# Samples' states as moving operands, head sums in column groups, rates in row halves: one change to the RWKV stage of a hybrid decoder step

## The chip, the core and the metric

The kernel runs on one core of one Trainium2 chip. The metric is the device time of one execution, in microseconds; the median of three runs of the kernel before is 1292.83 us (1290.94 to 1293.05). The engines are TensorE (PE, its weight loads shown as PEld), VectorE (DVE), ScalarE (ACT), GpSimd (POOL) and SyncE (SP), which issues most loads. Each engine takes its instructions in the order in which the program has them.

## The reference

Two layers, each a half SwiGLU block, a mixer and a second half SwiGLU block; the first mixer is RWKV-7, the second RetNet. There are 256 prompt rows and 8 sample rows (one new token each, with its own stored state), together 264 columns, and 16 heads of 64. The change lies in the RWKV mixer:

```python
kk = hd(k * k_k)
kk = kk / jnp.maximum(jnp.sqrt(jnp.sum(kk * kk, axis=-1, keepdims=True)), 1e-12)   # lengths
w_log = -softplus(-(w0 + jnp.tanh(xw @ w1) @ w2)) - 0.5                            # rates
a = sigmoid(a0 + (xa @ a1) @ a2)                                                   # rates
def step(S, inp):                      # S: value x key, one per sequence and head
    sa = jnp.einsum('bhvk,bhk->bhv', S, -kk_t)
    S = S * d_t + sa[..., None] * (kk_t * a_t) + v_t[..., None] * k_t
    return S, jnp.einsum('bhvk,bhk->bhv', S, r_t)
y = head_norm(y) * lnx_g + lnx_b
y = y + jnp.sum(r_h * k_h * r_k, axis=-1, keepdims=True) * v_h                     # bonus sums
```

## The kernel before

Activations lie with the 1024 channels on partitions: eight tiles `f` of 128 channels (two heads) by 264 columns. Weights stream from memory in units of eight 128x128 tiles. Outside the RWKV mixer each unit is split into two float32r parts (`hi` on ACT, `lo` on DVE) and a product takes three float32r matmuls (`mm3`, line 251). In the mixer the weights of k, r and v are used whole in float32, where one matmul is two records in the trace.

`weave` (line 204) runs the main `stream` and a list of side generators against a small model of engine clocks, and the tile scheduler then sets each engine's final order. In `rwkv` (line 464) the stream makes k, r and v (products `xk`, `xr`, `xv`), then the output product. Beside it run: `lengths` (707), sums of squares over a head, for four tiles a call; `rates` (721), which makes decay and `a` from 64 hidden rows each; `stage` (753), which spreads the lengths back over channels and makes `al`, `be`, `ka`; `inverse` (796), a DVE chain that inverts the 32x32 blocks of all heads and starts when every tile's `A` is there; `prep` (842), which makes the bonus products `bon` (tile `rc`) after the inverse; `heads2` (867), chunk products for two tiles a call; and `decode` (1034), the eight samples.

In `decode` each of 64 states (tile f and sample b, two heads each, value on one axis and key on the other) is the stationary operand and two columns of `dq` move (line 1058): 128 matmuls, 64x64 weights, two columns. The states come in four loads of 512 KB on POOL's queue into tiles of the tag `big`, three buffers, which `selT`, `V` and `tm` of the inverse use before them.

A sum over a head is a float32 matmul with a 0/1 matrix: `hsel` gives 16 rows (one a head) for the lengths, `selT` spreads them over 128 rows (763), `bones` sums and spreads at once for the bonus (947).

Of the kernel before, what the change touches and what calls it, by code (L numbers as in the profile page):

```python
# [10 lines left out]
F32 = mybir.dt.float32  # L11
F32R = mybir.dt.float32r
# [6 lines left out]
KT = D // 128  # L19
# [22 lines left out]
class Step:  # L42
# [158 lines left out]
    def mark(self, key):  # L201
        self.done[key] = self.now
# [242 lines left out]
class Rwkv(Step):  # L445
    def rw_consts(self, p):

        nc = self.nc
        c = p.tile([128, NCST], F32, name="cst")
        nc.scalar.dma_start(c, self.io["cst"])  # L450
        self.ident = c[:, CST["ident"]:CST["ident"] + 128]
        self.bones = c[:, CST["bones"]:CST["bones"] + 128]
        self.hsel = c[:, CST["hsel"]:CST["hsel"] + 128].rearrange("p (f h) -> p f h", f=KT)
# [7 lines left out]
        self.diag = col("diag", 4)  # L461
        self.rst = col("rst", 256)

    def rwkv(self, gain):
# [6 lines left out]
        with ExitStack() as ctx:  # L471
# [8 lines left out]
            same = dict(vT="mx", yl="lw", z2="kkn", z0="ta")  # L480

            def tmp(name, n=T, bufs=2):
                tag = same.get(name, name)
                return P.tile([128, n if tag in ("bs", "mv", "sd4", "nm4") else SLOT], F32, tag=tag, name=name, bufs=bufs)[:, 0:n]

            def parts(x, where="mm"):
                h, l = (slot("part", T, F32R) if w == "m" else
# [14 lines left out]
            selT = big("selT")[0:16].rearrange("p (f n) -> p f n", f=KT)  # L502
            nc.scalar.dma_start(selT, self.io["selT"])

            X = P1.tile([128, 32, 64], F32, name="X")
            for p0 in (32, 96):
# [131 lines left out]
            def heads():  # L638
                for p in range(KT // 2):
                    self.beside(TU["head"] + TU["headf"] * p, heads2(p))  # L640
                self.beside(TU["decode"], decode())

            def mixes(name, mu):
                if TU["wait_" + name]:
# [62 lines left out]
            def lengths(g, sqs):  # L707
                yield f"k{g}"
                ssq = ps_()
                for j in range(4):  # L710
                    self.mm(ssq[0:16, 0:T], self.hsel[:, 4 * g + j, :], sqs[j], j == 0, j == 3)
                rn = tmp("mx")[0:16]
                self.act(rn, ssq[0:16, 0:T], AF.Sqrt)
                self.ts(rn, rn, 1e-12, None, ALU.max)
                rnr[g] = slot("rnr")[0:16]
                self.vec("reciprocal", rn, out=rnr[g])
                mark(f"rn{g}")
                yield


            def rates():
                yield "hid"
                for f in range(KT):
                    s_ = st[f]
                    wh, wl = wa2[f]
                    (th, tl) = hid[0]
                    zw, za = ps_()[:, 0:T], ps_()[:, 0:T]
                    for z, p0 in ((zw, 0), (za, 64)):
# [24 lines left out]
            def stage(f):  # L753
# [88 lines left out]
            def prep(f):  # L842
# [11 lines left out]
                mark(f"bon{f}")  # L854
                yield

            def values(f, pv):
# [9 lines left out]
            def heads2(p):  # L867
# [74 lines left out]
                Ta = [c64(t[:, 256:448], NC - 1) for t in WT]  # L942

                for f, s_ in zip(fs, s2):
                    yield f"bon{f}"
# [88 lines left out]
            def decode():  # L1034
# [16 lines left out]
                Ss = [load(i) for i in range(3)]  # L1051
                yield 8.0
                po = ps_()[:, 0:128].rearrange("p (n q) -> p n q", q=2)
                for i in range(4):
                    for n in range(16):
                        f, b = divmod(16 * i + n, NS)
                        for e in range(2):
                            self.mm(po[own(e), 16 * i + n], Ss[i][own(e), n], dq[own(e), 1:5:3, f, b], behind=(n, e) != (0, 0))
                    if i == 0:
                        Ss.append(load(3))  # L1060
                    if i == 2:
                        yield 4.0
                self.act(fl(1), po[:, :, 0])
# [6 lines left out]
                self.tt(y[:, 0], y[:, 0], po[:, :, 1], ALU.add)  # L1070
# [55 lines left out]
    return slice(NV * i, NV * i + NV), slice(NV * i * 64, NV * (i + 1) * 64)  # L1126


NM = 60
NW = 10  # L1130
TU = dict(PEF=1.0, DVEF=1.0, ACTF=1.5, LP=0.5, LD=0.12, LA=0.15, SLACK=0.2, AHEAD=1, wk='mm', wr='mm', wv='mm', IL=8, pin_stream=0, pin_hidden=1, pin_rates=0, pin_mixes=0, pin_lengths=0, pin_stage=0, pin_inverse=0, pin_prep=1, pin_head=0, pin_saved=0, vp='r7', hv=0, hw=1, hidden=8, rates=7, mixr=1, mixv=5, inverse=0, saved=4, prep=3, head=2, headf=0.01, decode=9, lengths=3, stage=7, by_step=0, HE=0, wait_r=None, wait_v='k0', PW=4, SW=8, RK=3, INVY=8, pre=3.5, n0=3, n1=4)
WHOLE = "krv"
SLOT = 266


CST = {}
_c = 0
for _k, _w in (("ident", 128), ("bones", 128), ("hsel", 128), ("m_ak", 64), ("m_up", 64), ("eye2", 64), ("centre", 128),
               ("rows64", 64), ("back", 256), ("diag", 4), ("rst", 256)):
    CST[_k] = _c  # L1140
    _c += _w
NCST = _c
# [2 lines left out]
def consts():  # L1145
# [11 lines left out]
    hs = np.zeros((128, KT, 16))  # L1157
    for f in range(KT):
        hs[p, f, 2 * f + h] = 1
    put("hsel", hs.reshape(128, 128))  # L1160

    put("m_ak", q[:, None] < s)
    put("m_up", q[:, None] <= s)
# [9 lines left out]
    put("rows64", r64.reshape(128, 64))  # L1173
    put("back", bk.reshape(128, 256))
    put("diag", p[:, None] // 32 == np.arange(4)[None, :])
    r = np.ones((128, 4, 64))
    r[:, :, 0] = 0
    put("rst", r.reshape(128, 256))
    sel = np.zeros((16, KT, 2, 64), np.float32)
    for f in range(KT):  # L1180
        for e in range(2):
            sel[2 * f + e, f, e] = 1
    return c, sel.reshape(16, KT, 128)


def pack_wkv(s):
# [363 lines left out]

# [34 lines left out]
```

## Time and profile before

| | us |
|---|---|
| median of three runs | 1292.83 |
| the profiled execution | 1295.7 |
| its span | 1293.9 |
| PE busy in the span | 1266.0 |
| DVE busy | 850.0 |
| ACT busy | 673.8 |

A row of a timeline gives start, duration, engine, line, operation, output and inputs, and how many records are merged; the durations of neighbours overlap, so what a block costs is the distance from its start to the start of the next. The column PEclk in the windows is the granted clock of TensorE as a share of its full 2.4 GHz; 0.50 is its lower level, 1.2 GHz. The RWKV mixer lies between about 200 and 430 us.

### The profile page before, as it was taken

The numbers are of one execution on the slowest core, as the hardware profiler recorded it, in microseconds if no ns is written. First come the engines' busy times: TensorE is split into PE (matmuls) and PEld (weight loads), VectorE is DVE, ScalarE is ACT, GpSimd is POOL, SyncE is SP. The second block draws the span as 40 slices with busy tenths as digits, with TensorE's granted clock in tenths as the row PEclk, the third lists the DMA queues.
The fourth block names the chain that finished last, engine by engine and source line by source line (L and its number), as shares of the span: only waits on it lengthen the run. The fifth ranks groups of instructions, "written<-read, shape, count | busy, mean of one in ns | idle before, by whom it ended". The sixth has DMA issues, their size and how long they took to land.

```text
span 1293.9 us, 29072 instructions
## 1 busy us (share of the span) xinstructions
PE 1266.0 (98%) x12186; PEld 1197.3 (93%) x12186; DVE 850.0 (66%) x1391; ACT 673.8 (52%) x1167; POOL 67.3 (5%) x169
## 2 busy tenths in 40 slices
PE   9999999999998999999999999999999999999996
PEld 9999998678787999999999999988888799999996
DVE  6766567589235787765566665577878866666554
ACT  6544442653434677764456454445765554544542
POOL 0000001131100000000000000011111100000000
PEclk9999999999879999999999999999999999999998
DMA  7656554333400467665558555669879655555552
GB/s 233 181 181 185 181 170 137 99 116 115 147 7 23 153 219 222 211 195 182 178 179 279 183 181 182 204 236 329 312 269 334 213 194 180 179 180 179 179 180 83
DMA packets 66755, 239.09 MB, mean 185 GB/s; under 512 B 7504, under 2 KB 8912, under 8 KB 66496
## 3 DMA queue, kind: packets, MB, share of 16 engines
q1 hardware_dynamic: 59472, 212.63, 51.1%
q0 software_dynamic: 6544, 23.40, 4.9%
q8 instruction: 95, 1.56, 0.5%
q10 hardware_dynamic: 608, 1.21, 0.2%
q14 instruction: 36, 0.29, 0.1%
HBM read 214.86 MB, written 22.35 MB: 183 GB/s over the span
## 4 chain that ended last, share of the span: by engine, by line
PE 91%; DVE 4%; DMA 2%; ACT 2%; issue 1%; DVEq 0%; SPq 0%; ACTq 0%
PE ps L138 90%; DMA S<-in_ret 1%; DVE V L105 1%; DVE tm L105 1%; PE ps L153 1%; DMA rcst<-in_rcst 1%; DVE lo L105 0%; ACT X L90 0%; ACT L90 0%; ACT hi L90 0%; DMA raw<-in_w 0%; DVE KQ L105 0%; DVE xf L105 0%; ACT sd L90 0%; DVE sd L126 0%
## 5 line engine op out<-in xcount | busy, mean ns | idle before, releaser
L90 ACT ACTIVATE hi<-raw 128x1024 fp32r<-128x1024 f32 (+1 forms) x344 | 362.8, 1055 | 440.4 <-PE ps L138 207.9
L105 DVE TENSOR_TENSOR lo<-raw,hi 128x1024 fp32r<-128x1024 f32 (+1 forms) x344 | 418.5, 1217 | 233.6 <-ACT hi L90 232.3
L138 PE MATMUL ps<-ah,hi 128*128 128x264 f32 (+1 forms) x1824 | 522.9, 289 | 1.0 <-ACT ah L90 1.0
L138 PE MATMUL ps<-al,hi 128*128 128x264 f32 (+1 forms) x1824 | 517.1, 285 | 0.0
L138 PE MATMUL ps<-ah,lo 128*128 128x264 f32 (+1 forms) x1824 | 514.3, 285 | 0.0
L138 PEld LDWEIGHTS ps<-ah,hi 128*128 128x128 f32 x1824 | 342.8, 189 | 9.1 <-issue 7.4
L138 PEld LDWEIGHTS ps<-al,hi 128*128 128x128 f32 x1824 | 343.7, 189 | 4.1 <-issue 2.9
L138 PEld LDWEIGHTS ps<-ah,lo 128*128 128x128 f32 x1824 | 342.3, 189 | 0.1
L138 PE MATMUL ps<-hh,hi 128*128 128x264 f32 x832 | 237.2, 285 | 0.0
L138 PE MATMUL ps<-hl,hi 128*128 128x264 f32 x832 | 237.0, 285 | 0.0
L138 PE MATMUL ps<-hh,lo 128*128 128x264 f32 x832 | 236.8, 285 | 0.0
L138 PEld LDWEIGHTS ps<-hl,hi 128*128 128x128 f32 x832 | 156.8, 188 | 0.0
L138 PEld LDWEIGHTS ps<-hh,lo 128*128 128x128 f32 x832 | 156.7, 188 | 0.0
L138 PEld LDWEIGHTS ps<-hh,hi 128*128 128x128 f32 x832 | 156.4, 188 | 0.1
L105 DVE TENSOR_TENSOR h<-s,ps 128x264 f32<-128x264 f32 x88 | 37.1, 428 | 49.7 <-PE ps L138 48.3
L105 DVE TENSOR_TENSOR t<-ps,rs 128x264 f32<-128x264 f32 x88 | 37.2, 431 | 20.2 <-PE ps L138 19.9
L114 DVE SCALAR_TENSOR_TENSOR S<-ps,ks,S 128x512 f32<-128x512 f32 x64 | 45.0, 743 | 6.2 <-PE ps L138 6.2
L90 ACT ACTIVATE S<-S 128x1024 f32<-128x1024 f32 x32 | 33.8, 1056 | 14.3 <-DMA S<-in_ret 14.1
L105 DVE TENSOR_TENSOR hl<-h,hh 128x264 fp32r<-128x264 f32 x88 | 37.0, 427 | 0.3
L90 ACT ACTIVATE hh<-h 128x264 fp32r<-128x264 f32 x88 | 35.3, 408 | 3.6 <-DVE h L105 3.6
L90 ACT ACTIVATE s<-t 128x264 f32<-128x264 f32 x88 | 35.2, 409 | 2.2 <-DVE t L105 2.1
L138 PE MATMUL ps<-part,hi 128*128 128x264 f32 (+1 forms) x176 | 34.5, 309 | 0.0
(261 smaller groups left out, 1214.6 us busy)
## 6 DMA issues: line engine op xcount, KB each, us to landing
raw<-in_w SPq DMA_DIRECT2D x363, 512.0 KB, 3.6
S<-in_ret SPq DMA_DIRECT2D x32, 512.0 KB, 5.8
out_sret<-S POOLq DMA_DIRECT2D x32, 512.0 KB, 3.8
dS<-in_wkvt POOLq DMA_DIRECT2D x4, 512.0 KB, 4.4
Sd<-in_wkv SPq DMA_DIRECT2D x4, 512.0 KB, 4.7
out_swkv<-Sd POOLq DMA_DIRECT2D x4, 512.0 KB, 4.0
out_pret<-so POOLq DMA_DIRECT2D x8, 256.0 KB, 2.3
rcst<-in_rcst SPq DMA_DIRECT2D x1, 1100.0 KB, 6.9
```

The source lines that it names most:

```text
L90: ins = self.nc.scalar.activation(out=out, in_=in_, func=func, scale=scale, **kw)
L105: ins = self.nc.vector.tensor_tensor(out=out, in0=a, in1=b, op=op)
L114: ins = self.nc.vector.scalar_tensor_tensor(out=out, in0=a, scalar=s, in1=b, op0=op0, op1=op1)
L138: ins = self.nc.tensor.matmul(out=out, lhsT=lhsT, rhs=rhs, start=start, stop=stop)
L153: self.nc.tensor.transpose(out, in_, ident)
```

## The change

Four edits. `lengths` and the new `bonuses` sum squares and bonus products of four tiles into four 32-row column groups of one output (`rows64`, 128x32 weights) and keep the sums as two float32r parts; `to_heads` spreads them back with two float32r matmuls of 32 rows (`spread`), where `selT` and `bones` did it in float32. `rates` alternates its six float32r matmuls between the upper and the lower 64 rows. In `decode` the state is now the moving operand (64 columns), and the weight is a 64x32 tile of `kkr` that holds the two vectors of one state in its own two columns and zeros elsewhere; 16 states are added up in one output, four such outputs lie in four column groups, and `pick` turns the result back. The states pass in two halves of two loads each; `kkr` takes the third `big` buffer and `selT` is gone.

```diff
+            spread = P1.tile([128, 128], F32R, name="spread")
+            self.act(spread, self.back[:, 0])
+            def sums(out, xs):
+                for j, x in enumerate(xs):
+                    self.mm(out[32 * j:32 * j + 32, 0:T], self.rows64[:, 0], x, behind=j > 0)
+            def to_heads(out, rows, j):
+                s = slice(32 * j, 32 * j + 32)
+                for i, x in enumerate(rows):
+                    self.mm(out, spread[s], x[s], i == 0, i == 1)
...
                 ssq = ps_()
-                for j in range(4):
-                    self.mm(ssq[0:16, 0:T], self.hsel[:, 4 * g + j, :], sqs[j], j == 0, j == 3)
+                sums(ssq, sqs)
...
+                self.vec("reciprocal", rn, out=rn)
+                rnr[g] = parts(rn, "aa")
...
-                    for z, p0 in ((zw, 0), (za, 64)):
-                        s = slice(p0, p0 + 64)
-                        self.mm(z, wh[s], th[s], True, False)
-                        self.mm(z, wh[s], tl[s], False, False)
-                        self.mm(z, wl[s], th[s], False, True)
+                    for i, (w, t) in enumerate(((wh, th), (wh, tl), (wl, th))):
+                        for z, p0 in ((zw, 0), (za, 64)):
+                            s = slice(p0, p0 + 64)
+                            self.mm(z, w[s], t[s], i == 0, i == 2, behind=i + p0 > 0)
...
-                self.mm(rb, selT[:, f, :], rnr[f // 4])
+                to_heads(rb, rnr[f // 4], f % 4)
...
+            def bonuses(g):
+                for j in range(4):
+                    yield f"bon{4 * g + j}"
+                pr = ps_()
+                sums(pr, [st[4 * g + j]["bon"] for j in range(4)])
+                h, l = tmp("bh", T, 2, F32R), tmp("bl", T, 2, F32R)
+                self.act(h, pr[:, 0:T], scale=64.0)
+                self.stt(l, pr[:, 0:T], 64.0, h, ALU.mult, ALU.subtract)
...
-                    self.mm(pbo, self.bones, s_["bon"])
+                    to_heads(pbo, bonus[f // 4], f % 4)
...
-                        for e in range(2):
-                            self.mm(po[own(e), 16 * i + n], Ss[i][own(e), n], dq[own(e), 1:5:3, f, b], behind=(n, e) != (0, 0))
+                for h in range(2):
+                    K = big("kkr")
+                    nc.gpsimd.memset(K, 0.0)
+                    Ss = [load(2 * h + j) for j in range(2)]
+                    for q in range(2):
+                        nc.gpsimd.tensor_copy(K.rearrange("p (j n) -> p j n", j=2)[:, :, q:512:34],
+                                              fl(1 + 3 * q)[:, 32 * h:32 * h + 32].rearrange("p (j n) -> p j n", j=2))
+                    K = K.rearrange("p (j n m) -> p j n m", j=2, m=32)
+                    yield TU["dS"]
+                    pr = ps_()[:, 0:64]
                     for n in range(16):
+                        for j in range(2):
+                            for e in range(2):
+                                g = 64 * j + 32 * e
+                                self.mm(pr[g:g + 32], K[own(e), j, n], Ss[j][own(e), n], n == 0, n == 15, behind=(n, j, e) != (0, 0, 0))
+                    self.act(y[:, h], pr)
+                    yield 0.2
+                    for e in range(2):
+                        self.mm(po[own(e), :, 32 * h:32 * h + 32], y[:, h], self.pick[:, e])
```

The schedulers put many instructions elsewhere. TensorE's order around the end of the inverse, before (`tm,AT` is the inverse's first product, `PI,ka` and `cst,vt` belong to the first two tiles of `heads2`):

```order
L138 MATMUL ps<-cst,al 64x64 x24
L138 MATMUL ps<-xv,raw 128x264 x25
L138 MATMUL ps<-tm,AT 32x32 x32
L138 MATMUL ps<-xv,raw 128x264
L138 MATMUL ps<-PI,ka 64x64 x16
L138 MATMUL ps<-cst,vt 64x64 x16
```

and now:

```order
L138 MATMUL ps<-cst,al 64x64 x24
L138 MATMUL ps<-xv,raw 128x264
L138 MATMUL ps<-PI,ka 64x64 x16
L138 MATMUL ps<-cst,vt 64x64 x16
L138 MATMUL ps<-xv,raw 128x264 x17
L138 MATMUL ps<-rc,cst 32x264 x4
L138 MATMUL ps<-xv,raw 128x264 x4
L138 MATMUL ps<-tm,AT 32x32 x32
```

The first bonus sums (`rc,cst`) now stand ahead of the inverse's first product, with four value products between them. Before the last `be,al` block 48 of the 64 `xr` products now stand, where 40 stood.

TensorE's order around the samples' states, before (`G,Ls` and `Ly,G` are the chunk recurrence, `dq,dS` the states):

```order
L138 MATMUL ps<-al,ka 64x64 x16
L138 MATMUL ps<-pp,ka 64x64 x16
L138 MATMUL ps<-dq,dS 64x2 x96
L138 MATMUL ps<-G,Ls 64x64 x4
L138 MATMUL ps<-Ly,G 64x64 x4
L138 MATMUL ps<-rc,cst 128x264
L138 MATMUL ps<-PI,be 64x64 x16
```

and now:

```order
L138 MATMUL ps<-dS,kkr 32x64 x64
L138 MATMUL ps<-z,X 64x64 x16
L138 MATMUL ps<-aT,X 64x64 x12
L138 MATMUL ps<-al,ka 64x64 x16
L138 MATMUL ps<-pp,ka 64x64 x16
L138 MATMUL ps<-cst,yd 64x2x32 x2
L138 MATMUL ps<-G,Ls 64x64 x4
L138 MATMUL ps<-Ly,G 64x64 x4
L138 MATMUL ps<-bh,spread 128x264
L138 MATMUL ps<-bl,spread 128x264
L138 MATMUL ps<-PI,be 64x64 x16
```

The states stand ahead of the second head pair's products instead of behind them, and come as 64 and 64 matmuls instead of 96 and 32.

POOL's order from the last gather on, now (before, the first load stood where the first memset stands, and each of the other three loads waited for its own buffer):

```order
L1081 MEMSET kkr 128x1024
L1084 COPY kkr<-dq 128x2x16 x2
L110 TENSOR_TENSOR PI<-cst,PL 128x256 x4
L696 COPY dq<-vt 128x8 x6
L1073 DMA dS<-in_wkvt 128x1024
L696 COPY dq<-vt 128x8 x2
L1073 DMA dS<-in_wkvt 128x1024
L110 TENSOR_TENSOR PI<-cst,PL 128x256 x2
L1081 MEMSET kkr 128x1024
L1073 DMA dS<-in_wkvt 128x1024 x2
L1084 COPY kkr<-dq 128x2x16 x2
```

The first load takes the buffer of `tm`, the second that of `V`, whose last reader is the inverse's last product (`V,AT`). The second memset and the last two loads wait for the first 64 matmuls.

## Rows read from the trace of the kernel before

**Rows 1.** The page: busy time of each engine, and the chain that ended last

```profile
PE 1266.0 (98%) x12186; PEld 1197.3 (93%) x12186; DVE 850.0 (66%) x1391; ACT 673.8 (52%) x1167; POOL 67.3 (5%) x169
...
PE 91%; DVE 4%; DMA 2%; ACT 2%; issue 1%; DVEq 0%; SPq 0%; ACTq 0%
```

**Rows 2.** Windows: stretch, us, busy PE PEld DVE ACT POOL, PEclk, DMA share, GB/s

```profile
250.00:282.00 32.00, 32.00 (x460) 22.56 (x459) 28.87 (x74) 23.63 (x64) 14.18 (x43) 1.00 0.22 71
...
348.00:349.00 1.00, 0.33 (x6) 0.33 (x8) 0.00 (x0) 0.00 (x0) 0.00 (x0) 0.70 0.31 123
...
349.00:365.00 16.00, 16.00 (x289) 14.47 (x287) 1.81 (x7) 0.66 (x2) 1.79 (x3) 0.50 0.12 36
...
369.00:372.00 3.00, 3.00 (x111) 2.88 (x107) 2.40 (x12) 0.00 (x0) 0.00 (x0) 0.50 0.01 3
...
423.00:428.00 5.00, 5.00 (x25) 4.76 (x26) 3.72 (x8) 1.69 (x3) 0.00 (x0) 0.66 0.00 0
...
440.00:490.00 50.00, 50.00 (x411) 49.93 (x410) 39.80 (x56) 39.20 (x95) 0.54 (x1) 1.00 0.67 214
```

**Rows 3.** TensorE's timeline, samples' states: start, us, what, records, idle before

```profile
348.67 10.40 PE L138 MATMUL ps<-dq,dS 64*64 64x2 f32 x191 [2.29 <-issue]
...
358.83 0.77 PE L138 MATMUL ps<-G,Ls 64*64 64x64 f32 x8
...
365.99 1.98 PE L138 MATMUL ps<-dq,dS 64*64 64x2 f32 x64
```

**Rows 4.** DVE's timeline, either end of the inverse's chain

```profile
283.84 1.97 DVE L132 STREAM_TRANSPOSE A<-Ag 128x1024 f32<-128x1024 f32 x1 [1.41 <-ACT Ag L90]
...
318.17 1.71 DVE L114 SCALAR_TENSOR_TENSOR rc<-rc,par,k 128x264 f32<-128x264 f32 x4
```

**Rows 5.** TensorE's timeline, from the value products to the second head pair

```profile
307.30 11.39 PE L138 MATMUL ps<-xv,raw 128*128 128x264 f32 x50
...
318.62 1.20 PE L138 MATMUL ps<-tm,AT 32*32 32x32 f32 x64
...
336.48 1.16 PE L138 MATMUL ps<-rc,cst 128*128 128x264 f32 x4
...
344.40 0.69 PE L138 MATMUL ps<-z,X 64*64 64x64 f32 x32
```

**Rows 6.** TensorE's timeline, a block of 64x32 weights and its successor

```profile
254.69 0.73 PE L138 MATMUL ps<-be,al 64*32 64x32 f32 x48
...
255.35 0.71 PE L138 MATMUL ps<-rnr,selT 16*128 16x264 f32 x2
```

**Rows 7.** POOL's timeline, two loads of the states

```profile
336.86 0.53 POOL L1048 DMA_DIRECT2D dS<-in_wkvt  x1 [0.74 <-PE ps L138]
...
352.55 0.59 POOL L1048 DMA_DIRECT2D dS<-in_wkvt  x1 [6.94 <-PE ps L138]
```

**Rows 8.** Tile dS, its loads

```profile
DMA to landing us min/median/max: 4.2/4.4/5.2
```

**Rows 9.** Line 799, a memset of 128x1024 on POOL: duration ns min/median/max

```profile
L799 POOL MEMSET V<- x1: 963/963/963, 204.5 to 204.5; 128x1024 f32 x1
```

**Rows 10.** TensorE's timeline, one bonus sum and its successor

```profile
381.63 0.71 PE L138 MATMUL ps<-rc,cst 128*128 128x264 f32 x2
...
382.28 0.69 PE L138 MATMUL ps<-PI,be 64*64 64x64 f32 x32
```

**Rows 11.** TensorE's timeline, lengths' sums and one pair of rates

```profile
240.70 1.96 PE L138 MATMUL ps<-sq,cst 128*16 128x264 f32 x8
...
242.59 1.60 PE L138 MATMUL ps<-xk,raw 128*128 128x264 f32 x6
...
263.33 0.51 PE L138 MATMUL ps<-part,hi 64*128 64x264 f32 x4
...
263.90 0.71 PE L138 MATMUL ps<-rnr,selT 16*128 16x264 f32 x2
```

More of the change, by code (lines that the diff above doesn't have):

```diff
@@ L461, in rw_consts @@
         self.diag = col("diag", 4)
+        self.pick = col("pick", 128).rearrange("p (e q n) -> p e q n", e=2, q=2)
         self.rst = col("rst", 256)
@@ L478, in slot, with tmp @@
                 return P.tile([128, SLOT], dt, tag=tag, name=name, bufs=bufs or NM)[:, 0:n]
-            same = dict(vT="mx", yl="lw", z2="kkn", z0="ta")
-            def tmp(name, n=T, bufs=2):
+            same = dict(z2="kkn", z0="ta", bh="kkn", bl="ta")
+            def tmp(name, n=T, bufs=2, dt=F32):
                 tag = same.get(name, name)
-                return P.tile([128, n if tag in ("bs", "mv", "sd4", "nm4") else SLOT], F32, tag=tag, name=name, bufs=bufs)[:, 0:n]
+                return P.tile([128, SLOT], dt, tag=tag, name=name, bufs=bufs)[:, 0:n]
             def parts(x, where="mm"):
@@ L641, in heads @@
                 self.beside(TU["decode"], decode())
+                self.beside(TU["prep"], bonuses(0), bonuses(1))
             def mixes(name, mu):
@@ L709, in lengths @@
                 ssq = ps_()
-                for j in range(4):
-                    self.mm(ssq[0:16, 0:T], self.hsel[:, 4 * g + j, :], sqs[j], j == 0, j == 3)
-                rn = tmp("mx")[0:16]
-                self.act(rn, ssq[0:16, 0:T], AF.Sqrt)
+                sums(ssq, sqs)
+                rn = tmp("mx")
+                self.act(rn, ssq[:, 0:T], AF.Sqrt, scale=64.0)
                 self.ts(rn, rn, 1e-12, None, ALU.max)
-                rnr[g] = slot("rnr")[0:16]
-                self.vec("reciprocal", rn, out=rnr[g])
+                self.vec("reciprocal", rn, out=rn)
+                rnr[g] = parts(rn, "aa")
                 mark(f"rn{g}")
@@ L855, in prep @@
                 yield
+            bonus = [None, None]
+            def bonuses(g):
[6 more added lines that the diff above has]
+                self.stt(l, pr[:, 0:T], 64.0, h, ALU.mult, ALU.subtract)
+                bonus[g] = h, l
+                mark(f"bonus{g}")
+                yield
             def values(f, pv):
@@ L944, in heads2 @@
                 for f, s_ in zip(fs, s2):
-                    yield f"bon{f}"
+                    yield f"bonus{f // 4}"
                     pbo = ps_()[:, 0:T]
-                    self.mm(pbo, self.bones, s_["bon"])
+                    to_heads(pbo, bonus[f // 4], f % 4)
                     self.tt(s_["bon"], pbo, s_["vt"])
@@ L1049, in load @@
                     return S
[L1051 to L1054, printed above, removed]
-                    for n in range(16):
-                        f, b = divmod(16 * i + n, NS)
-                        for e in range(2):
-                            self.mm(po[own(e), 16 * i + n], Ss[i][own(e), n], dq[own(e), 1:5:3, f, b], behind=(n, e) != (0, 0))
[L1059 to L1063, printed above, removed]
+                po = ps_()[:, 0:128].rearrange("p (q n) -> p q n", q=2)
+                for h in range(2):
[8 more added lines that the diff above has]
+                    pr = ps_()[:, 0:64]
+                    for n in range(16):
+                        for j in range(2):
[6 more added lines that the diff above has]
+                        self.mm(po[own(e), :, 32 * h:32 * h + 32], y[:, h], self.pick[:, e])
+                self.act(fl(1), po[:, 0])
                 pbr = ps_()[:, 0:128].rearrange("p (q n) -> p q n", q=2)
@@ L1126, in part_of @@
     return slice(NV * i, NV * i + NV), slice(NV * i * 64, NV * (i + 1) * 64)
-NM = 60
+NM = 61
 NW = 10
-TU = dict(PEF=1.0, DVEF=1.0, ACTF=1.5, LP=0.5, LD=0.12, LA=0.15, SLACK=0.2, AHEAD=1, wk='mm', wr='mm', wv='mm', IL=8, pin_stream=0, pin_hidden=1, pin_rates=0, pin_mixes=0, pin_lengths=0, pin_stage=0, pin_inverse=0, pin_prep=1, pin_head=0, pin_saved=0, vp='r7', hv=0, hw=1, hidden=8, rates=7, mixr=1, mixv=5, inverse=0, saved=4, prep=3, head=2, headf=0.01, decode=9, lengths=3, stage=7, by_step=0, HE=0, wait_r=None, wait_v='k0', PW=4, SW=8, RK=3, INVY=8, pre=3.5, n0=3, n1=4)
+TU = dict(PEF=1.0, DVEF=1.0, ACTF=1.5, LP=0.5, LD=0.12, LA=0.15, SLACK=0.2, AHEAD=1, wk='mm', wr='mm', wv='mm', IL=8, pin_stream=0, pin_hidden=1, pin_rates=0, pin_mixes=0, pin_lengths=0, pin_stage=0, pin_inverse=0, pin_prep=1, pin_head=0, pin_saved=0, vp='r7', hv=0, hw=1, hidden=8, rates=7, mixr=1, mixv=5, inverse=0, saved=4, prep=3, head=2, headf=0.01, decode=9, lengths=3, stage=7, by_step=0, HE=0, wait_r=None, wait_v='k0', PW=4, dS=5.0, SW=8, RK=3, INVY=8, pre=3.5, n0=3, n1=4)
 WHOLE = "krv"
@@ L1137 @@
 _c = 0
-for _k, _w in (("ident", 128), ("bones", 128), ("hsel", 128), ("m_ak", 64), ("m_up", 64), ("eye2", 64), ("centre", 128),
-               ("rows64", 64), ("back", 256), ("diag", 4), ("rst", 256)):
+for _k, _w in (("ident", 128), ("bones", 128), ("m_ak", 64), ("m_up", 64), ("eye2", 64), ("centre", 128),
+               ("rows64", 64), ("back", 256), ("diag", 4), ("pick", 128), ("rst", 256)):
     CST[_k] = _c
@@ L1156, in consts @@
     put("bones", h[:, None] == h[None, :])
[L1157 to L1160, printed above, removed]
     put("m_ak", q[:, None] < s)
@@ L1175, in consts @@
     put("diag", p[:, None] // 32 == np.arange(4)[None, :])
+    pk = np.zeros((2, 2, 2, 8, 2, 2, 2, 2, 2, 8))
+    for j, e, i, b, q in np.ndindex(2, 2, 2, 8, 2):
+        pk[j, e, i, b, q, e, q, j, i, b] = 1
+    put("pick", pk.reshape(128, 128))
     r = np.ones((128, 4, 64))
@@ L1178, in consts @@
     put("rst", r.reshape(128, 256))
[L1179 to L1183, printed above, removed]
+    return c
 def pack_wkv(s):
@@ L1552 @@
     inp = {k: np.asarray(v) for k, v in inputs.items()}
-    cst, selT = consts()
+    cst = consts()
     rcst = ret_consts()
@@ L1556 @@
         x=pack_x(np.concatenate([inp["x_prompt"][0], inp["x_sample"][:, 0]], 0)),
-        par=pack_par(inp), cst=cst, selT=selT, rcst=rcst,
+        par=pack_par(inp), cst=cst, rcst=rcst,
         shift=pack_x(inp["state_rwkv_shift"][0]),
```

5 lines of the change are left out of this document (1 added, 4 removed).

## The prediction

> **What bounds the kernel now.** I read first the page's engine table and its chain: TensorE is busy 98% of the span and carries 91% of the chain that ended last [rows 1]. Time is won only where TensorE has less to do, waits less or runs at a better clock. All edits lie in the RWKV mixer, so next come the windows there. TensorE has its full clock nearly everywhere, 411 float32r matmuls of 264 columns in 50 us, or 0.12 us each, but from 349 to 365 us the granted clock is 0.50, the lower level of 1.2 GHz, again from 369 to 372, and 0.66 in the mean of 423 to 428 [rows 2]. TensorE's timeline says what stands there: behind an idle time of 2.3 us, 191 records of the samples' states take 10.2 us, and 64 more come at 365.99 [rows 3]. The third view is DVE's: busy for 28.9 of the 32 us from 250 to 282 [rows 2], then in the inverse's chain from 283.84 on, and only at 318.17 does it begin the four bonus products `rc` that follow the inverse [rows 4]. TensorE's row there reads as a tie: value products run without a gap from 307.30 to 318.62, and the inverse's first product follows at once [rows 5]. So up to 318 us two chains are about equally late, TensorE's and DVE's, and behind that TensorE is alone.
>
> **The samples' states.** Before, they take 346.20 (348.67 less the 2.3 idle and a first record of 0.2) to 358.83, 12.6 us, and 2.0 at 365.99: 14.6 us [rows 3]. After, there are 128 matmuls, 256 records, with 64x32 weights and 64 moving columns on four quarters of the array. The nearest row is the block `be,al`, also 64x32 weights on the same quarters, 48 records in 0.66 us, start to start, 13.8 ns each [rows 6]: 3.5 us for 256. It moves only 32 columns; I take 15 ns, 3.8 us. The other end is the states' own price at full clock, 64 records in 1.98 us, 31 ns [rows 3]: 7.9 us. The turning back by `pick`, four small products, I put at 0.5 us in all. So 4.3 us against 14.6.
>
> Two statements of the Trainium skill speak against 15 ns. TensorE: Matmul & The Clock Gate, section Back-to-back issue gap, gives matmuls of 1 to 64 columns about 60 cycles each, some 25 ns; 256 of them would be, as an estimate from that page, 6.4 us. TensorEngine Tiling (Array Packing), Gotcha 1, says that row tiles may not use one PSUM bank at once, and both row halves of the new product write one bank; by that rule pairs would run in turn, near the 31 ns end. The block `be,al` does the same, both halves into one bank, and took 13.8 ns a record [rows 6], so the trace agrees with neither.
>
> **The new waits for loads.** The first two loads are issued ahead of the first half, the second of them into the buffer of `V`, which the inverse's last product frees. Before, such a load was issued 0.4 us after that product's end (336.48, then 336.86) [rows 5, 7], and it lands 4.4 us after issue, 4.2 to 5.2 [rows 8]: 4.8 us. TensorE's work in between is four spreads at 0.12 [rows 2] and the first pair's 0.85 and 2.0 us of chunk products, 3.3 us. It waits 1.5 us (1.3 to 2.3), and all of `heads2` queues behind it, since TensorE is strictly in order. The second half waits longer: only after the first half does POOL clear `kkr`, 0.96 us [rows 9], and issue two loads at 0.55 [rows 7], so the last one lands 0.1 + 0.96 + 1.1 - 0.55 + 4.4 plus some sharing, 6.0 to 7.4 us, I take 7.0, after the first half's end. TensorE has meanwhile 1.8 us of the second pair's products and what stood between 358.83 and 365.99: 7.2 us at half clock [rows 3], 3.6 at full, less two bonus sums at 0.65 [rows 10], plus four spreads, 0.5, and `pick`. That is 4.9 us; the wait is 2.1 (1.1 to 2.5).
>
> **Lengths, spreads, rates.** A float32 sum costs 0.47 us (four in 1.89, 240.70 to 242.59) [rows 11]. In four column groups side by side four cost about one, so `lengths` saves 1.4 us on its first call; in its second other products stand between, and I count nothing. Eight spreads by `selT` have the columns of a bonus sum, 0.65 us [rows 10], and become two of 0.12 each: 8 x 0.41, 3.3 us. Six matmuls of a rate take 0.57 us, 263.33 to 263.90 [rows 11]; in alternating halves three times 0.12, 8 x 0.21, 1.7 us (none if the halves take turns). TensorE sheds 6.4 us before the inverse starts.
>
> What of that reaches the end? DVE is nearly full there [rows 2], and the first spread comes 1.4 us plus three rates, 2.0 us, sooner, so the inverse starts about 2.0 us earlier (1.4 to 2.9: DVE also gets one more subtraction for each call of `lengths`, 0.4 us as a quarter of the `rc` row [rows 4]). TensorE meanwhile runs ahead of it. The reordered queue puts 54 products of `xr` and `xv` between the last `be,al` and the first bonus sums, where 65 stood ahead of the inverse's first product: 11 x 0.453 (25 in 11.32 [rows 5]) is 5.0 us less, 1.2 us of `PI,ka` and `cst,vt` more. So TensorE reaches those sums at 318.62 - 3.8 - 2.0 = 312.8, but all four `rc` are ready at 318.17 + 1.71 - 2.0 = 317.9 [rows 4]. It stands idle 5 us with the inverse's product queued behind. An idle of 2.3 us went ahead of the drop at 348.7 [rows 2, 3], so I expect half clock when it resumes; in the dense products of 423 to 428 a drop lost 5 x 0.34 = 1.7 us [rows 2].
>
> From there: before, 318.62 to 344.40 where the second pair's products begin [rows 5], 25.8 us, of which 0.6 is idle. After: less two bonus sums (1.0 us), plus four spreads (0.5), two grouped sums (0.9), three `xv` (1.4), less 1.2 done already: 25.8 us. So 317.9 + 25.8 + 1.7 = 345.4, 1.0 later than the like point before. The 6.4 us are gone, eaten by the idle time.
>
> **The sum.** After: 345.4, wait 1.5, first half 1.9, work 4.9, wait 2.1, second half 1.9, hence 357.7; before the same work ends at 365.99 + 1.98 = 368.0. That is 10.3 us. The half clock of 369 to 372 should be gone, 1.5 us [rows 2]. Four later bonus sums go from 0.65 to 0.24, 1.6 us; TensorE has gaps there, so I count 0.8. Together 12.6 us off the profiled execution: 1295.7 - 12.6 = 1283.1. That execution, span 1293.9 plus 1.8 around it, stands 2.9 us above the median, so in the median's terms 1280.2, and I say 1280. What follows is feed-forward work at TensorE's pace, where a start that is earlier by so much ends earlier by as much. The constants and the extra slot of `NM` I cost at nothing: they issue nothing of their own.
>
> **Rivals.**
> - The clock holds at the long wait, or the waits for loads are short: the 1.7 us come back, and up to 3 of the waits. For it: behind the idle time of 346 stood products of two columns, so the idle alone need not have been the cause. Against it: 5 us is over twice as long. 1275.5 to 1278.5.
> - The clock falls at the first load wait and stays down over the samples' stage, as it did for 16 us before [rows 2]. The 8.7 us of work there double, the second wait of 2.1 vanishes: 6.6 us lost, 1286.6. Against it: the new products are denser.
> - The tiles take turns, so that the change doesn't do what it says: 31 ns for the states, 4.1 us, and bonus sums at four times 0.47, 2.9 us: 1287. `be,al` speaks against it [rows 6]. Slower rates alone would only shorten the idle 5 us.
> - The slower side: the 5 us stall at the bonus sums puts the clock down, and the small products behind it, cut up by the waits for loads, don't bring it back before the second half is done. All 34.5 us of work from 317.9 on then cost double; the waits vanish (3.6) and the 1.7 counted already fall out: 29 us, 1309. It decides once the half level costs over 14.4 us of work, some 29 us on end. The longest stretch so far is 16, under products of two columns.
>
> **Chances.** Forecast 0.55 (1278.5 to 1284, its term bounds); better 0.13; half clock at the samples 0.13; tiles in turn 0.10; slower side 0.04; 0.05 for a loss that I don't see and that leaves the time as it was. Range: 1275 to 1288, which takes in the first three rivals but for their ends. A measurement here tells 0.2%, 2.6 us, from no change. Faster 0.89, same 0.06, slower 0.05.
>
> **What would show it.** In the profile after: an idle time of TensorE of some 5 us ahead of `rc,cst` with 32 rows, released by DVE's `rc`; half clock just behind it; `dS,kkr` in two blocks of 128 records, 1.9 us each, with 1.5 and 2.1 us of waiting for loads ahead; full clock at 369 to 372 less 10. The forecast is wrong if the blocks take 4 us each, if the clock in the samples' stage is 0.50, or if the inverse starts later than 283 us.

## The result: 0.75% slower, and what the profile after shows

The changed kernel takes 1301.58 us (median of four, 1299.79 to 1303.49) against 1292.03; the ratio is 1.0075 with the 95% interval [1.0061, 1.0090]. The forecast was 1280, in a range of 1275 to 1288; the change went the other way. The profiled execution took 1302.58 us, span 1300.8, against 1293.9 before. The page after, the engines' busy time and the chain that ended last, answers [rows 1]:

```profile
PE 1259.2 (97%) x12210; PEld 1189.6 (91%) x12210; DVE 849.4 (65%) x1395; ACT 675.6 (52%) x1174; POOL 69.9 (5%) x175
...
PE 90%; DVE 4%; DMA 2%; ACT 1%; issue 1%; DVEq 0%; SPq 0%; POOL 0%; ACTq 0%
```

TensorE works 6.8 us less and the span is 6.9 us longer: 13.7 us more idle time. The windows of [rows 2] after, and one that is new (310 to 320):

```profile
250.00:282.00 32.00, 29.84 (x455) 21.81 (x455) 26.68 (x69) 22.43 (x60) 12.24 (x38) 1.00 0.24 70
310.00:320.00 10.00, 7.13 (x80) 6.16 (x81) 9.51 (x24) 1.78 (x2) 0.00 (x0) 0.83 0.18 52
349.00:365.00 16.00, 9.90 (x381) 8.80 (x381) 3.09 (x10) 3.07 (x9) 3.52 (x7) 0.89 0.40 134
369.00:372.00 3.00, 2.44 (x127) 2.21 (x128) 1.52 (x7) 0.22 (x1) 0.00 (x0) 1.00 0.02 5
```

From 250 to 282 and from 349 to 365 us TensorE had no idle time before; now it has 2.2 and 6.1 us, though from 349 to 365 the half clock is nearly gone (0.89 instead of 0.50). Ahead of the inverse, TensorE's timeline had this row for the last `be,al` before:

```profile
282.64 0.73 PE L138 MATMUL ps<-be,al 64*32 64x32 f32 x48
```

Now, ahead of and behind the inverse, answering [rows 5, 6]:

```profile
255.41 0.73 PE L138 MATMUL ps<-be,al 64*32 64x32 f32 x48 [1.68 <-DVE be L114]
...
281.08 0.51 PE L138 MATMUL ps<-part,spread 32*128 32x264 f32 x2
281.52 0.73 PE L138 MATMUL ps<-be,al 64*32 64x32 f32 x48
282.18 3.83 PE L138 MATMUL ps<-xr,raw 128*128 128x264 f32 x16
285.94 0.73 PE L138 MATMUL ps<-be,al 64*32 64x32 f32 x48
...
312.87 0.89 PE L138 MATMUL ps<-PI,ka 64*64 64x64 f32 x26 [3.01 <-DVE M L105]
...
314.65 8.71 PE L138 MATMUL ps<-xv,raw 128*128 128x264 f32 x34
323.29 0.65 PE L138 MATMUL ps<-rc,cst 128*32 128x264 f32 x8
323.87 2.05 PE L138 MATMUL ps<-xv,raw 128*128 128x264 f32 x8
325.85 1.20 PE L138 MATMUL ps<-tm,AT 32*32 32x32 f32 x64
...
343.96 1.20 PE L138 MATMUL ps<-V,AT 32*32 32x32 f32 x64
345.09 0.39 PE L138 MATMUL ps<-bh,spread 32*128 32x264 f32 x2
```

DVE's timeline, answering [rows 4]:

```profile
287.14 1.98 DVE L132 STREAM_TRANSPOSE A<-Ag 128x1024 f32<-128x1024 f32 x1 [2.94 <-ACT Ag L90]
...
320.72 1.70 DVE L114 SCALAR_TENSOR_TENSOR rc<-rc,par,k 128x264 f32<-128x264 f32 x4
```

The last `be,al` comes 3.3 us later than before, and so does the inverse. TensorE then stops at `PI,ka` for an `M` that stands inside the inverse's chain on DVE, resumes at less than full clock (0.83 in that window), and reaches `tm,AT` 7.2 us later than before, 5.1 behind the start of `rc` where it was 0.5. `V,AT` ends 8.6 us later (345.09, before 336.48). The samples' stage on TensorE's timeline, answering [rows 3]:

```profile
353.07 0.28 PE L138 MATMUL ps<-M,WT 64*64 64x64 f32 x3 [4.11 <-issue]
...
354.81 3.20 PE L138 MATMUL ps<-dS,kkr 64*32 64x64 f32 x124 [0.94 <-DMA dS<-in_wkvt]
...
360.44 0.46 PE L138 MATMUL ps<-pp,ka 64*64 64x64 f32 x14 [0.65 <-issue]
...
365.97 0.68 PE L138 MATMUL ps<-cst,al 64*64 64x64 f32 x16 [1.41 <-issue]
366.58 1.77 PE L138 MATMUL ps<-dS,kkr 64*32 64x64 f32 x112
369.52 0.43 PE L138 MATMUL ps<-dS,kkr 64*32 64x64 f32 x16 [1.17 <-issue]
...
372.87 0.46 PE L138 MATMUL ps<-cst,vt 64*64 64x64 f32 x17 [0.91 <-issue]
```

The states end at 369.9, 2.0 us later than before. The first block of 124 records took 3.1 us (354.81 to 357.95), the second 1.8 for 112: behind the gap of 4.11 and the wait for the load the clock had fallen to its half level.

```profile
354.80:357.40 2.60, 2.59 (x100) 2.59 (x104) 0.00 (x0) 0.01 (x1) 0.00 (x0) 0.50 0.00 0
```

From 336 to 430 us, idle time that no row releases ("issue") sums to 11.3 us in 9 pieces, against 2.7 in 2. The pieces have a beat: 126, 128 and 127 matmul records lie between the gaps that end at 360.44, 365.97, 369.52 and 372.87, each with its weight load. The profile's DMA table has a queue of kind "instruction":

```profile
q8 instruction: 96, 1.57, 0.5%
```

That is 16.4 KB a packet, or some 65 bytes for each of the 252 to 256 records between two gaps. The trace also has the time of each packet. The nine gaps end 1.2 to 1.5 us behind the end of a q8 packet: the gap that ends at 365.97 behind a packet that ended at 364.64, for instance, and the one at 369.52 behind 368.23. The same holds for all 84 such gaps from 336 to 430 us in the twenty traces of this case, with 1.2 to 1.6 us, and the 2.29 us ahead of the states before is one of them (348.67, packet 347.41). So "issue" is here TensorE waiting for its instructions. In 345 to 350 us, ahead of the gap of 4.11, the table for that stretch has no row for q8 (no packet starts between 344.55 and 350.74), and the weight queue q1 takes 86% of the time of the 16 DMA engines:

```profile
q1 hardware_dynamic: 337, 1.25, 86.4%
```

That the weight loads held the packet up is likely by this, but no run took them away. Where gaps follow each other at full clock, 128 and 127 records take 3.55 and 3.35 us, 27 ns each; the 126 ahead of them, with spreads of 264 columns among them, took 5.53.

### The profile page after: what moved, and what is told of

Its sections match the earlier page's. It is cut to its first block, busy times and chain, and to the rows that moved or that the text cites. A ratio compares the mean times of both kernels' runs of the same rounds, so it can differ in the third digit from the quotient of the medians.

```text
span 1300.8 us, 29135 instructions
## 1 busy us (share of the span) xinstructions
PE 1259.2 (97%) x12210; PEld 1189.6 (91%) x12210; DVE 849.4 (65%) x1395; ACT 675.6 (52%) x1174; POOL 69.9 (5%) x175
## 4 chain that ended last, share of the span: by engine, by line
PE 90%; DVE 4%; DMA 2%; ACT 1%; issue 1%; DVEq 0%; SPq 0%; POOL 0%; ACTq 0%
PE ps L138 89%; PE ps L153 1%; DVE V L105 1%; DVE tm L105 1%; DMA dS<-in_wkvt 1%; DMA raw<-in_w 1%; DMA rcst<-in_rcst 1%; DMA S<-in_ret 0%; ACT hi L90 0%; DVE lo L105 0%; ACT L90 0%; DVE KQ L105 0%; DVE xf L105 0%; DVE A L132 0%; DVE on L120 0%
```

## Experiments

Each ran beside the kernel before, whose median was 1291.5 to 1292.2 us each time. The edits are shown shortened.

**States alone**, and its counterpart: the changed `decode` in the kernel before, and the old one in the changed kernel.

```diff
 # kernel before
+ new decode(), pick
 # changed kernel
- new decode()
+ old decode()
```

> The kernel before with the new samples' states alone (lengths, spreads, bonus sums and rates as before). Theory A: the states are a gain of their own, the loss comes from the reordered queue ahead of and behind the inverse, which this kernel does not have; the inverse starts at 283.8 us as before, the stretch from V,AT to the end of the states is shorter by 6.6 us as in the changed kernel: 1285 to 1287. Rival B: what is lost comes from the states' own side (late loads, idle time that the profile puts on issue, a longer tail): 1291 to 1295.

> The changed kernel with the samples' states as in the kernel before (64x64 weights, two columns); lengths, spreads, bonus sums and rates as changed. Theory A: this part carries the loss; second V,AT ends some 8 us later than before, some 1 us of it comes back in the later bonus sums: 1298 to 1301. Rival B: this part is neutral, 1290 to 1294.

Measured 1288.04, ratio 0.9969 [0.9956, 0.9982], and 1302.85, 1.0097 [1.0074, 1.0119]. The states are a gain of 4 us in the kernel before, smaller than theory A gave; the loss lies in the rest, and is larger than it gave. The states alone on TensorE's timeline:

```profile
343.31 1.97 PE L138 MATMUL ps<-dS,kkr 64*32 64x64 f32 x123
348.35 0.31 PE L138 MATMUL ps<-dS,kkr 64*32 64x64 f32 x5 [3.07 <-issue]
...
356.99 1.98 PE L138 MATMUL ps<-dS,kkr 64*32 64x64 f32 x124 [1.41 <-DMA dS<-in_wkvt]
```

A block takes the 2 us of the forecast where its instructions are there, and a gap splits the first.

**Rates in the old order**, in the changed kernel.

```diff
-  for i, (w, t) in enumerate(((wh, th), (wh, tl), (wl, th))): for z, p0 in ((zw, 0), (za, 64)): ...
+  for z, p0 in ((zw, 0), (za, 64)): three products
```

> The changed kernel with the rates' six products in the order of before (three of one half of the rows, then three of the other). Theory A: alternating the halves brought nothing (0.56 us a pair of rates after, 0.57 before): within 1 us of the changed kernel, 1300.5 to 1302.5. Rival C: the halves do pass side by side and the gain is 1.7 us ahead of the inverse, so that going back costs it: 1303 to 1304.

1297.77, 1.0048 [1.0036, 1.0061]: outside both, and faster by 3.8 than with the new rates. A pair of rates takes as long in either order (further below), so it is not their own time. In the trace the first `be,al` waits 0.68 us here where it waited 1.68, and the gap of 4.11 is 1.89. Counted from the first sum of the lengths, the two traces are 0.5 us apart at the end of `V,AT` and 3.0 at the end of the states, so most of it comes with that gap; what links the gap to the rates no run shows.

**Half as many matmuls for the states**, in the changed kernel and in the kernel before: all 128 rows, four columns a state.

```diff
-  self.mm(pr[g:g + 32], K[own(e), j, n], Ss[j][own(e), n], n == 0, n == 15, ...)       # 128 of them
+  self.mm(pr[32*j:32*j+32], K[:, j, n], Ss[j // 2][:, 8 * (j % 2) + n], n == 0, n == 7, ...)  # 64
```

> The changed kernel with half as many matmuls for the samples' states: 128 rows by 32 columns of weights, both heads of a state at once in four columns of their own, 64 matmuls instead of 128. Theory D: the idle time that the profile puts on issue is a bound on how fast instructions reach TensorE (a gap after about 125 matmul records); with 128 records fewer two gaps or some 2 to 3 us fall out of 345 to 372 us: 1298 to 1300. Rival E: the gaps belong to something else (a load, the clock), and the records cost the same each: a gain of 128 records at 14 to 25 ns less what waits anyway, 0 to 1 us: 1300.5 to 1302.

> The kernel before with the new samples' states alone, in half as many matmuls (128x32 weights, both heads of a state in four columns of their own). Theory D (instructions reach TensorE too slowly in dense small products): from the end of V,AT to the last product of rd it takes 2 to 3 us less than the 78.9 us of the same edit with 128 matmuls: 1285 to 1286. Rival E (the columns that pass decide, 14 to 25 ns a record, and the waits for loads stay): within 1 us of it, 1287 to 1288.5.

1296.61, 1.0041 [1.0027, 1.0054]: 5 us better than the changed kernel, more than either theory gave. On the kernel before 1286.50, 0.9958 [0.9944, 0.9973], between the two theories and not to be told from the 128 matmuls (1288.04).

**Early loads**, on the last kernel: `kkr` in `Ag` and `A3`, which the inverse has done with, so that `big` holds loads alone.

```diff
+  Ks = Ag, A3 (cleared and filled on POOL); loads = [load(0)]
+  yield "X0"; loads.append(load(1)); yield "X1"; loads.append(load(2))
```

> The same as the one before it, TensorE's order unchanged, but the two-column weights lie in buffers that the inverse has done with, and both loads of the first half are issued before or just behind the inverse's end. Theory F: the late loads cost: the wait of 1.4 us ahead of a half of the states and part of the idle time put on issue go: 1282 to 1284.5. Rival G: the time put on issue takes the place of the wait, since the same instructions have to come; 1285 to 1287, less than 1 us from the kernel with late loads.

1283.37, 0.9936 [0.9922, 0.9951], the fastest of all: 8.7 us below the kernel before. Theory F holds. The waits for loads are gone; from 336 to 372 us three gaps of the other kind stay, 3.6 us in all, two of them shown. TensorE's timeline:

```profile
342.97 1.10 PE L138 MATMUL ps<-dS,Ag 128*32 128x64 f32 x64
...
346.78 0.75 PE L138 MATMUL ps<-al,ka 64*64 64x64 f32 x29 [1.05 <-issue]
...
352.36 0.57 PE L138 MATMUL ps<-pp,be 64*64 64x64 f32 x23 [2.01 <-issue]
352.87 1.10 PE L138 MATMUL ps<-dS,A 128*32 128x64 f32 x64
```

**The same with 128 matmuls again**, loads and place unchanged (the diff of two experiments ago, reversed).

> The best kernel so far (1283.4) with the states in 128 matmuls of 64x32 weights instead of 64 of 128x32, same loads, same place. Theory D: the supply of instructions bounds the dense small products, some 3.5 us for 125 matmul records; 128 records more cost 1.5 to 3.5 us: 1285 to 1287. Rival E: they cost their 14 ns each at most and fall into waits: 0 to 1 us, 1283 to 1284.5.

1285.17, 0.9954 [0.9938, 0.9969]: the median is on theory D's side, but the intervals overlap. The traces say 4.6 us of issue idle in 336 to 372 against 3.6. That instructions are waited for is what the rows show; what it costs is measured only to within the noise.

**Lengths and spreads alone**, in the kernel before.

```diff
+  sums(ssq, sqs) ... rnr[g] = parts(rn, "aa")
+  to_heads(rb, rnr[f // 4], f % 4)
```

> The kernel before with the lengths' sums in column groups and their spreads in two float32r parts alone; rates, bonus sums and states as before. Theory A: this alone turns the order of the last be,al blocks and the idle of 3 us ahead of PI,ka, so the inverse starts at 286 to 287 (283.8 before) and the kernel takes 1294 to 1297. Rival I: the shorter spreads bring 2 to 3 us and the delay comes from the rates and bonus sums: 1288 to 1291.

1301.58, 1.0078 [1.0064, 1.0093], 9.5 us slower: as much as the whole change, and beyond both theories. Its trace has the same two marks on TensorE, more strongly:

```profile
311.67 0.77 PE L138 MATMUL ps<-PI,ka 64*64 64x64 f32 x26 [3.37 <-DVE M L105]
...
352.41 0.37 PE L138 MATMUL ps<-M,WT 64*64 64x64 f32 x3 [5.47 <-issue]
```

**Bonus sums held, `PI,ka` held, both.** My first theory was that what stands ahead of `tm,AT` costs what it waits.

```diff
+  yield f"X{g}"     # in bonuses, ahead of sums(): run 1 and 3, changed kernel
+  yield "T0"        # in heads2, ahead of PI,ka; T0 = behind the first tm,AT: run 2 (lengths alone) and 3
```

> The changed kernel with one wait added: the bonus sums of a half are ordered behind the inverse's last product of that half, so that tm,AT stands directly behind the value products, as before. Theory A: of the 8.6 us by which V,AT ended later, 3.9 came from the bonus sums and value products ahead of tm,AT; V,AT ends at 340 to 342 instead of 345.1 and the kernel takes 1297 to 1299. Rival H: TensorE only waits elsewhere (3 us ahead of PI,ka stay, and the sums now stand behind), V,AT 344 or later: 1300.5 to 1302.

> The kernel before with the new lengths and spreads alone, as in the run of that edit (1301.6), but PI,ka of the first pair held behind the inverse's first product tm,AT, where it stood before. Theory J: the loss is TensorE's wait of 3.4 us ahead of PI,ka for DVE's M, which stands behind the inverse's chain, and the half clock that follows over the value products; without them V,AT ends at 338 to 340 instead of 342.8 and the kernel takes 1293 to 1297. Rival K: the late start of the inverse (285.65 instead of 283.84) and the stretch behind V,AT carry the loss: 1299 to 1302.

> The changed kernel with both held back: PI,ka of the first pair behind tm,AT, and the bonus sums of a half behind that half's last product of the inverse. Theory J: V,AT ends at 339 to 341 instead of 345.1, no half clock ahead of tm,AT: 1295 to 1298. Rival K: 1300 to 1302, as with the sums held alone (1301.7).

1301.74, 1301.71 and 1304.42: nothing won, and the third is slower than either theory gave. In the second run's trace `tm,AT` starts at 319.22 and `V,AT` ends at 336.94, within 0.6 us of before, so the wait at `PI,ka` was cured; then ACT's timeline reads

```profile
337.86 1.06 ACT L90 ACTIVATE hi<-raw 128x1024 fp32r<-128x1024 f32 x1 [3.88 <-DMA raw<-in_w]
...
340.01 1.21 ACT L90 ACTIVATE z<-ps 128x256 f32<-128x256 f32 x4
```

and TensorE's

```profile
340.45 1.28 PE L138 MATMUL ps<-z,X 64*64 64x64 f32 x30 [3.51 <-ACT z L90]
```

ACT takes its instructions in order and waits 3.88 us for a weight load, with what TensorE needs behind it. The theory fell: one wait is cured and the next takes its place.

**The price of a spread.** `weave` writes its order by the model in `mm`, which prices a float32r matmul of 264 columns at 0.11 us; a spread's two are 0.23 there, where `selT` was 0.44. (In the trace after, a spread takes 0.44 us.) Only this number is changed, in the lengths alone, then in the changed kernel.

```diff
-  self.mm(out, spread[s], x[s], i == 0, i == 1)
+  self.nc.tensor.matmul(out=out, lhsT=spread[s], rhs=x[s], start=i == 0, stop=i == 1)
+  self.spent("pe", 0.22, out, spread[s], x[s])
```

> The kernel before with the new lengths and spreads alone (1301.6), and one number changed: the planner's clock model prices a spread's two matmuls at 0.22 us each instead of 0.11, together what selT had. By that alone TensorE's order of be,al, xr, xv, tm,AT, PI,ka and V,AT is that of the kernel before. Theory N: the loss is the order: 1290 to 1293. Rival O: the new operations themselves lose it (the first be late, one more DVE and ACT instruction a call): 1298 to 1302.

> The changed kernel with the price of a spread in the planner's model at 0.22 us a matmul and nothing else changed. Theory N: the last be,al and PI,ka stand where they stood, only the bonus sums still stand ahead of tm,AT; most of the loss goes: 1288 to 1294. Rival O: 1299 to 1302.

1294.18, 1.0028 [1.0015, 1.0042]: of the 9.5 us over the kernel before 2.7 are left, so some 7 were order, with the same operations. DVE's timeline of this run:

```profile
283.62 1.98 DVE L132 STREAM_TRANSPOSE A<-Ag 128x1024 f32<-128x1024 f32 x1 [1.94 <-ACT Ag L90]
```

The inverse starts 42.9 us behind the first sum of the lengths (at 240.73), where it was 43.1 before: in the old order the cheaper operations bring it 0.2 us forward, not 2.0, and TensorE now waits for DVE's `be` four times, 1.8 us in all. Of what is left, the trace shows a wait of 2.7 us for ACT's `WT`. In the changed kernel the new price gives 1299.94, 1.0070 [1.0049, 1.0092], theory O's range and not to be told from the changed kernel itself: the bonus sums still stand ahead of `tm,AT` there and wait 2.2 us for `rc`.

**The rest of the lengths**, on the early loads: the same edit, then with one swap on ACT.

> The best kernel so far (states in 64 matmuls, early loads; 1283.4) with the new lengths and spreads in the order of before (price 0.22). Theory N with TensorE as the bound: 8 x 0.2 us of spreads and 1.3 us of sums less, partly hidden behind DVE: 1281 to 1283.4. Rival P: DVE and its chain bound the start of the inverse, so the shorter products bring nothing and one more split a call costs up to 1 us: 1283.4 to 1285.

> The kernel with early loads and the new lengths in the old order of TensorE (1287.5), with ACT's WT of the first pair ahead of the weight split hi that it stood behind; TensorE's order stays. Theory N: the wait of 2.3 us for WT goes, and with it the loss: 1283.5 to 1285.5. Rival O: the new lengths cost it by themselves: 1287 to 1288.5.

1287.52, 0.9975 [0.9959, 0.9990], slower than both theories gave. ACT's timeline of this kernel, and TensorE's row that waits:

```profile
337.40 1.06 ACT L90 ACTIVATE hi<-raw 128x1024 fp32r<-128x1024 f32 x1 [4.39 <-DMA raw<-in_w]
338.36 0.96 ACT L90 ACTIVATE WT<-ps 128x448 f32<-128x448 f32 x2
```

```profile
338.94 0.94 PE L138 MATMUL ps<-bT,WT 64*64 64x64 f32 x22 [2.27 <-ACT WT L90]
```

The swap pins the two instructions:

```diff
+  self.tc.keep_in_program_order(ins)     # WT of the first pair, and hi of rw_g2 behind it
```

1284.62, 0.9946 [0.9935, 0.9958], 2.9 us better, as theory N gave; the two intervals only just part. `WT` of the first pair starts at 335.34 and its product doesn't wait. But TensorE waits as long for `WT` of the second pair, where the kernel without the swap had, one product on, an issue gap of 1.67:

```profile
352.62 1.06 PE L138 MATMUL ps<-PI,be 64*64 64x64 f32 x30 [2.33 <-ACT WT L90]
```

From the end of `V,AT` to the end of the states it takes 18.8 us here, 22.1 without the swap, and 18.4 with the early loads alone. What is left to the new operations, 1.2 us above 1283.37, is within the noise: no gain or loss of theirs is shown in this order.

**Rates, and bonus sums, on the early loads** (lengths as before).

> The kernel before with the new states in 64 matmuls and early loads (1283.4), and the rates' six products alternating between the row halves. Theory A: alternation of float32r row halves is worth nothing here; within 1 us, 1282.5 to 1284.5, and a pair of rates keeps 0.5 to 0.6 us. Rival C: pairs pass side by side, 0.2 us less a rate: 1281 to 1282.5.

> The same base (1283.4) with the bonus sums in column groups and two float32r parts, held behind the inverse; lengths and rates as before. Theory L: eight float32 sums of 0.65 us become two of 0.6 and sixteen of 0.12, about 2 us less TensorE work behind the inverse, where TensorE bounds: 1281 to 1282.5. Rival M: the sums come later than what they are needed for, ACT and DVE turns put in their place a wait: 1283.5 to 1286.

Rates: 1284.82, 0.9946 [0.9928, 0.9964], no gain, a little above theory A. A pair on TensorE's timeline, answering the last rows of [rows 11]:

```profile
263.31 0.51 PE L138 MATMUL ps<-part,hi 64*128 64x264 f32 x4
263.65 0.28 PE L138 MATMUL ps<-part,lo 64*128 64x264 f32 x2
263.87 0.71 PE L138 MATMUL ps<-rnr,selT 16*128 16x264 f32 x2
```

0.56 us, as before: six in 0.57 was already less than six times 0.12. Bonus sums: 1290.10, 0.9991 [0.9978, 1.0004], 6.7 us lost, more than rival M gave. TensorE's waits from 336 to 430 us in this kernel, then in the one without:

```profile
PE ps L138 <- issue: 6.7, 5, 1.9
```

```profile
PE ps L138 <- issue: 3.6, 3, 2.0
```

and its clock is low, where the other has 1.00:

```profile
350.00:358.00 8.00, 6.95 (x182) 6.25 (x183) 2.48 (x7) 1.64 (x4) 0.51 (x1) 0.61 0.24 70
```

**The changed kernel in the right order**: price, bonus sums behind the inverse, `WT` ahead of `hi`.

> The changed kernel, all four edits and their operations kept, with three changes of order only: a spread priced at 0.22 us in the planner's model, the bonus sums behind the inverse's last product of their half, and WT ahead of the weight split on ACT. Theory N: what it lost was order; the states' 4 us remain as gain, the bonus sums cost up to 3: 1287 to 1291. Rival O: the bonus sums and the waits at the states lose by themselves: 1293 to 1300.

1297.18, 1.0031 [1.0018, 1.0043], in rival O's range: order alone gives back 4.4 of 9.6 us. The executions spread from 1292.93 to 1299.16, and the trace, of the slowest, shows one reason ahead of the inverse, where no bonus sum stands:

```profile
255.86 1.10 PE L138 MATMUL ps<-be,al 64*32 64x32 f32 x48 [1.68 <-DVE be L114]
...
254.00:268.00 14.00, 12.32 (x127) 8.95 (x126) 10.60 (x25) 9.61 (x22) 4.16 (x13) 0.63 0.03 5
```

Behind the same wait of 1.68 us as in the changed kernel the clock falls, and the last `be,al` comes 45.2 us behind the first sum (41.9 before, 41.7 in the lengths alone at the right price). Seven traces have this wait; in five of them the granted clock of 254 to 268 us is 0.63 to 0.76, in two 1.00, the changed kernel's own among these. With the rates in the old order the wait is 0.68 and the clock 1.00. So part of the rest goes with the new rates and the clock; how much the bonus sums keep is not shown.

## Why the prediction was wrong

- **The inverse's start** is the step that failed: "the first spread comes ... 2.0 us, sooner, so the inverse starts about 2.0 us earlier". It came 3.3 later (`A` at 287.14), past the 283 named as the sign of a wrong forecast. The new order puts 48 `xr` products ahead of the last `be,al` where 40 stood. I counted these eight only as work gone from behind it, not as work in front of it: at 0.47 us each (16 records, or eight products, in 3.76 us, 282.18 to 285.94) they cost 3.8 us. TensorE also waited 2.2 us for DVE's `be`, which I had at nothing. Against these 6 us stand 1.3 won by the first sums and 1.4 by the spreads, which leaves the 3.3. Even in the old order, in the run with the lengths alone at the right price, only 0.2 of the 2.0 us came, with 1.8 us of waits for `be`. Lengths and spreads alone lost 9.5 us, some 7 of it by order; in the changed kernel order gave back 4.4 of 9.6.
- **The idle time of 5 us ahead of `rc,cst`** did not come: `rc,cst` at 323.29 follows a value product at once. TensorE stopped at `PI,ka` instead (3.01 us). That row stood in the new order; I had counted it as work already done, and not asked what it waits for. A lowered clock was forecast behind the other stall and came behind this one (0.83 from 310 to 320).
- **The states' 15 ns a record** were right at full clock: 112 in 1.77 us, 15.8 ns, into one PSUM bank from both row halves. The first block took 25 ns a record, most of it at half clock. That is the second rival, but it lasted some 3 us and not the whole stage. And the stage waits for instructions: two blocks of 127 records came at 27 ns a record, gaps included. Against the states' own 31 ns at full clock [rows 3] that is little. By these numbers most of the gain there was the half clock that went, as forecast (1.00 at 369 to 372); no run separates the two.
- **The load waits**, 1.5 and 2.1 forecast, were 0.94 and none; the gaps for instructions, which I had at nothing, stood in their place. That the second load came 1.2 us behind `V,AT`'s end (346.33) was POOL's doing, as the row of POOL shows, where a copy waits for ACT's `vt`:

```profile
345.42 0.97 POOL L696 COPY dq<-vt 128x8 f32<-128x8 f32 x1 [1.16 <-ACT vt L90]
346.33 0.54 POOL L1073 DMA_DIRECT2D dS<-in_wkvt  x1
```

- **Sums, spreads, rates.** The first four sums took 0.58 us (240.66 to 241.24 on TensorE's timeline, 1.89 before), 0.1 more than forecast. A spread's two matmuls take 0.44 us (281.08 to 281.52), not 0.24; the rates won nothing.
- **The sum**: 12.6 us off, made of a states' stage that begins 1.0 later and ends 10.3 earlier (it began 8.6 later, by `V,AT`, and ended 2.0 later), and of 2.3 behind it. Behind it 4.9 more were lost up to the span's end; issue idle from 372 to 430 us is 3.9 there, where it was 0.4. From 12.6 won to 6.9 lost is 19.5 us: 7.6 up to the end of `V,AT`, 4.7 in the states' stage, 7.2 behind it. So the inverse's start is the first step that failed and not the only one.
- Of the rivals, none had order or the supply of instructions as its mechanism. The slower side asked for half clock over all 34.5 us from 317.9 on; it came for some 3 us behind `PI,ka` and as long again at the first block. 0.05 stood for "a loss that I don't see".

Two statements weighed there can be set beside the rows. TensorE: Matmul & The Clock Gate of the Trainium skill, Back-to-back issue gap, would have given some 25 ns. The 15.8 ns above disagree; the 27 ns of the stretches with gaps and the 25 ns of the first block agree only by their size, since the one holds a wait and the other half clock. TensorEngine Tiling (Array Packing) of the Trainium skill, Gotcha 1, speaks against row tiles that share a bank. Here both row halves wrote one bank, in column groups of their own, at 15.8 ns a record.

Open: what in the bonus sums costs 6.7 us on the early loads. The traces show more issue idle (3.1 us) and a low clock over 8 us, but no run took either away alone. Open too: why the first rates' order moved 3.8 us, and how much of the changed kernel's loss the new rates' wait at the first `be,al` carries in executions where the clock falls behind it.

## What to carry over

Where a planner writes the order, price a new operation in its model at what the old one had and run that first: the same operations cost 9.5 us or 2.7. When products move away from behind a row, ask what they now stand in front of; here eight of them were counted once. Ask of each in-order queue what a moved instruction stands behind, on ACT and DVE as well, since cured waits reappear one row on. And count instructions in stretches of small products: half as many matmuls won 5 us in the changed kernel, though nothing clear of the noise in the two others.

## What was not expected of the hardware

- In dense stretches of small products TensorE stopped after about every 127 matmuls with their weight loads, for 0.7 to 4.1 us in the samples' stage, and went on 1.2 to 1.5 us behind the end of a 16.4 KB packet of the instruction queue; the longest stop stood where weight loads held 86% of the DMA engines' time. Two such blocks came at 27 ns a record.
- The same wait of 1.68 us left the clock at 1.00 in two traces and took it to 0.63 to 0.76, over 254 to 268 us, in five.
- A float32r matmul with 32x128 weights and 264 columns took 0.22 us, with 128x128 weights 0.12 [rows 2].
